# Gradient clipping by norm on one core: loads of all 128 partitions in row blocks of four, finer tail loads, one reduction matmul, fewer stores

## The chip, the cores and the metric

The kernel runs on one core of a Trainium2 chip. The metric is the device time of one execution in microseconds (us), lower is better. The fast runs of one kernel are spread over 0.05 to 0.75 us; times are given as medians with the range. The profile is one execution with the hardware profiler; its span is 1.8 us shorter than the time of the same run. On one core the granted TensorE clock was 1.00, so it plays no part.

## The reference

```python
def setup_inputs():
    batch, dim = 512, 4096
    return {"grad": np.random.randn(batch, dim).astype(np.float32) * 10, "max_norm": 1.0}

def reference(grad, max_norm):
    norm = np.sqrt(np.sum(grad ** 2))
    scale = min(1.0, max_norm / (norm + 1e-8))
    return (grad * scale).astype(np.float32)
```

8.39 MB come in from the HBM (the memory beside the core), are held in the SBUF (the memory in the core, here as tiles of 128 partitions), and 8.39 MB go out. The copying is done by the DMA engines, 16 by the page; a load or a store is issued on a queue, here that of SyncE (SP) or of ScalarE (ACT). No output can be scaled before the last input has been squared and summed, so there are three stages in a row: load, reduction, store.

## The kernel before

Block `t` of 128 rows goes to the 128 partitions, so a partition holds four rows of 16 KB. The first block is loaded in two pieces, by partitions: 16 and 112. ScalarE squares 9/16 of the columns of each piece (the first block as one piece), VectorE the rest; each writes a partial sum per partition into `acc`. The partial sums are summed per partition and a matmul with a matrix of ones adds over the partitions; the last 256 columns are squared by VectorE alone and added by a second matmul.

```python
    gt = g.rearrange("(t p) d -> t p d", p=P)
    ot = o.rearrange("(t p) d -> t p d", p=P)
    big = sb.tile([P, T, ncols], fp32)
    in_chunks = [
        (0, 0, ncols, 0, 16),          # block, columns, partitions
        (0, 0, ncols, 16, P),
        (1, 0, ncols, 0, P),
        (2, 0, ncols, 0, P),
        (t_last, 0, 2304, 0, P),
        (t_last, 2304, mid, 0, P),     # mid = 3840
        (t_last, mid, ncols, 0, P),
    ]
    for t, c0, c1, r0, r1 in in_chunks:
        nc.sync.dma_start(out=big[r0:r1, t, c0:c1], in_=gt[t][r0:r1, c0:c1])
    # ... ScalarE and VectorE square the pieces, partial sums into acc ...
    nc.vector.tensor_scalar(out=dumm[:, 0:ai], in0=acc[:, 0:ai], ..., accum_out=rowsum)
    nc.tensor.matmul(out=psum_tot, lhsT=ones, rhs=rowsum, start=True, stop=False)
    # ... VectorE squares the last 256 columns into acc[:, ai] ...
    nc.tensor.matmul(out=psum_tot, lhsT=ones, rhs=acc[:, ai : ai + 1], start=False, stop=True)
    nc.scalar.activation(out=qv, in_=psum_tot, func=ACT.Sqrt, scale=1.0 / (mn * mn))
    nc.vector.tensor_scalar(out=rq, in0=qv, scalar1=1.0, scalar2=None, op0=OP.max)
    nc.vector.reciprocal(out=s, in_=rq)
    # ... ten pieces: VectorE ("D") or ScalarE ("A") multiplies by s,
    #     and the SP or the ACT queue stores the piece ...
```

## Time and profile before

| | before |
|---|---|
| time | 53.87 us (4 runs, 53.60 to 54.04) |
| span of the profile | 52.0 us |
| VectorE, ScalarE busy | 26%, 37% |
| input packets on the DMA engines | 1.80 to 25.84 us |
| first scaling starts | 29.17 us |
| output packets | 30.42 to 50.78 us |

The packet times are read from the DMA packets in the trace, with the first input packet put at 1.80 us here and in every later table; on the clock of the timeline they are 0.02 us earlier in this kernel. The rest is from the page and the timeline. No engine is busy half of the time: the kernel is bound by its two DMA stages and by the serial reduction between them.

The first view is the page's part 2 of the kernel before: the span in 40 slices of 1.3 us, the busy tenths of the 16 DMA engines and the GB/s that they moved. The bytes of a packet are counted in the slice in which it starts, so single slices swing about the true rate.

```profile
DMA  0997798989999999999500069999999999999980
GB/s 0 202 202 202 202 365 239 290 327 416 453 453 428 416 416 390 411 413 425 200 0 0 0 217 406 447 428 388 405 421 411 460 422 428 403 403 409 453 346 0
```

The pair has to be read together. The engines count as busy from the second slice on, but in slices 2 to 5 they move 202 GB/s and only from about the tenth on over 410. A busy DMA engine is not always one that moves data at full rate: a packet of 16,384 bytes took 0.61 to 0.65 us later on, and 0.73 to 2.14 us in the slow stretch.

The second view is the chain of work that ended last, by engine (page, part 4). SPq, ACTq and DVEq are the instruction queues of SyncE, ScalarE and VectorE, PE is the matmul engine, and "issue" is time in which nothing was waited for that the profile shows.

```profile
DMA 44%; ACT 14%; issue 5%; SPq 4%; DVE 3%; PE 2%; ACTq 1%; DVEq 0%
...
```

The third view is the DMA list of the kernel before: the input loads, their KB, and the microseconds from issue to landing. The last load (128 KB, issued at 3.5 us) lands 22.8 us later, at 26.32.

```profile
big<-in_grad_dram SPq DMA_DIRECT2D x2, 2048.0 KB, 17.0
...
big<-in_grad_dram SPq DMA_DIRECT2D x1, 1792.0 KB, 10.5
...
big<-in_grad_dram SPq DMA_DIRECT2D x1, 128.0 KB, 22.8
```

The fourth is the timeline around the end of the input: start, duration, engine, line, operation, operands, and in brackets the idle time before it with what ended it.

```profile
11.75 2.12 ACT L83 ACTIVATE sq_a<-big 128x2304 f32<-128x2304 f32 x1 [9.53 <-DMA big<-in_grad_dram]
...
26.18 0.86 DVE L89 CUSTOM_DVE_ANT_0 sq_v<-big 128x672 f32<-128x672 f32 x1 [0.81 <-DMA big<-in_grad_dram]
26.96 0.42 DVE L113 CUSTOM_DVE_ANT_0 sq_v<-big 128x256 f32<-128x256 f32 x1
27.30 0.16 DVE L101 TENSOR_SCALAR_CACHE_REDUCE dumm<-acc 128x10 f32<-128x10 f32 x1
...
27.52 0.59 PE L110 MATMUL psum_tot<-rowsum,ones 128*128 128x1 f32 x2 [27.52 <-DVE dumm L101]
27.98 0.57 PE L123 MATMUL psum_tot<-acc,ones 128*128 128x1 f32 x2
28.58 0.17 ACT L127 ACTIVATE qv<-psum_tot 128x1 f32<-128x1 f32 x1 [1.50 <-PE psum_tot L123]
...
29.17 2.83 ACT L153 ACTIVATE big<-big,s 128x512 f32<-128x512 f32 x2 [0.42 <-DVE s L129]
```

The first square starts only at 11.75 us. At the end VectorE squares 672 and then 256 columns, sums (L101), and two matmul pairs follow each other. Note that the sum over the partial sums runs after the square of the last piece, although the program has them the other way round: the scheduler changed the order, and so the split into two matmuls hides less than was meant (0.22 us, by an experiment below).

### The profile page before, as it was taken

Reading aid. Unit: us, or ns where it says so; the run is one execution under the profiler, and the core shown is the slowest. Engines: PE = TensorE matmul, PEld = TensorE weight load, DVE = VectorE, ACT = ScalarE, POOL = GpSimd, SP = SyncE. Lnnn points to the kernel's source line nnn. Section 1 sums busy time; section 2 is a strip of 40 time slices with the busy share of each in tenths; the row PEclk is TensorE's granted clock in tenths of the full one; section 3 lists DMA queues with packets and bytes.
Section 4 is the critical chain, followed back from the end, with each engine's and each line's share of the span. In section 5 each row is a group of like instructions: output and inputs, shape, how many; then the busy total and the mean of one; then the engine's idle time right before and its main releaser. Section 6 shows DMA issues by size and latency. Waiting matters only on the chain.

```text
span 52.0 us, 127 instructions
## 1 busy us (share of the span) xinstructions
PE 1.0 (2%) x4; PEld 0.9 (2%) x4; DVE 13.7 (26%) x22; ACT 19.4 (37%) x18; POOL 0.2 (0%) x4
## 2 busy tenths in 40 slices
PE   0000000000000000000007000000000000000000
PEld 0000000000000000000007000000000000000000
DVE  1000000009602930495581899900000000000000
ACT  4600000009702940595670696999770000000000
POOL 1000000000000000000000000000000000000000
DMA  0997798989999999999500069999999999999980
GB/s 0 202 202 202 202 365 239 290 327 416 453 453 428 416 416 390 411 413 425 200 0 0 0 217 406 447 428 388 405 421 411 460 422 428 403 403 409 453 346 0
DMA packets 2320, 16.78 MB, mean 322 GB/s; under 512 B 272, under 2 KB 528, under 8 KB 912
## 3 DMA queue, kind: packets, MB, share of 16 engines
q1 hardware_dynamic: 1600, 12.19, 63.5%
q10 hardware_dynamic: 720, 4.59, 21.4%
HBM read 8.39 MB, written 8.39 MB: 322 GB/s over the span
## 4 chain that ended last, share of the span: by engine, by line
DMA 44%; ACT 14%; issue 5%; SPq 4%; DVE 3%; PE 2%; ACTq 1%; DVEq 0%
DMA big<-in_grad_dram 44%; ACT big L153 13%; SPq L75 4%; DVE sq_v L89 2%; ACTq L159 1%; PE psum_tot L110 1%; PE psum_tot L123 1%; ACT qv L127 0%; DVE s L129 0%; DVE rq L128 0%; DVE dumm L101 0%; DVE acc L113 0%; DVE sq_v L113 0%; DVEq L89 0%; DVE acc L89 0%
## 5 line engine op out<-in xcount | busy, mean ns | idle before, releaser
L83 ACT ACTIVATE sq_a<-big 128x2304 f32<-128x2304 f32 (+2 forms) x5 | 8.6, 1716 | 15.8 <-DMA big<-in_grad_dram 15.8
L89 DVE CUSTOM_DVE_ANT_0 sq_v<-big 128x1792 f32<-128x1792 f32 (+2 forms) x5 | 8.1, 1628 | 17.9 <-DMA big<-in_grad_dram 17.9
L153 ACT ACTIVATE big<-big,s 128x2048 f32<-128x2048 f32 (+2 forms) x5 | 8.7, 1783 | 1.3 <-ACT big L153 0.8
L161 DVE TENSOR_SCALAR big<-big,s 128x2048 f32<-128x2048 f32 (+2 forms) x5 | 4.6, 990 | 0.0
L77 ACT ACT_TABLE_LOAD x1 | 1.3, 1283 | 0.7 <-PEq L185 0.7
L110 PE MATMUL psum_tot<-rowsum,ones 128*128 128x1 f32 x2 | 0.6, 363 | 27.5 <-DVE dumm L101 27.5
L110 PEld LDWEIGHTS psum_tot<-rowsum,ones 128*128 128x128 f32 x2 | 0.5, 313 | 27.5 <-DVE dumm L101 27.5
L83 ACT ACTIVATION_READ_ACCUMULATOR sq_a<-big 128x1 f32 x5 | 0.9, 187 | 0.0
L127 ACT ACTIVATE qv<-psum_tot 128x1 f32<-128x1 f32 x1 | 0.2, 171 | 1.5 <-PE psum_tot L123 1.5
L123 PE MATMUL psum_tot<-acc,ones 128*128 128x1 f32 x2 | 0.6, 352 | 0.0
L123 PEld LDWEIGHTS psum_tot<-acc,ones 128*128 128x128 f32 x2 | 0.6, 336 | 0.0
L128 DVE TENSOR_SCALAR rq<-qv 128x1 f32<-128x1 f32 x1 | 0.2, 155 | 1.3 <-ACT qv L127 1.3
L113 DVE CUSTOM_DVE_ANT_0 sq_v<-big 128x256 f32<-128x256 f32 x1 | 0.4, 420 | 0.0
L89 DVE DVE_READ_ACCUMULATOR2_ANT acc<- 128x1 f32 x5 | 0.4, 82 | 0.0
L72 DVE MEMSET ones<- 128x128 f32 x1 | 0.2, 165 | 0.8 <-PEq L185 0.8
L77 ACT ACTIVATE junk<-ones 1x1 f32<-1x1 f32 x1 | 0.2, 203 | 0.0
L129 DVE RECIPROCAL s<-rq 128x1 f32<-128x1 f32 x1 | 0.2, 163 | 0.0
L101 DVE TENSOR_SCALAR_CACHE_REDUCE dumm<-acc 128x10 f32<-128x10 f32 x1 | 0.2, 158 | 0.0
L185 POOL MEMSET const-bfloat16-1.0<- 128x1 bf16 x1 | 0.1, 102 | 0.0
L185 POOL MEMSET const-uint8-127<- 128x1 uint8 x1 | 0.1, 102 | 0.0
L185 POOL MEMSET const-float32-0.0<- 128x1 f32 x1 | 0.1, 100 | 0.2 <-issue 0.2
L185 POOL MEMSET const-float32-1.0<- 128x1 f32 x1 | 0.1, 99 | 0.0
(2 smaller groups left out, 0.2 us busy)
## 6 DMA issues: line engine op xcount, KB each, us to landing
big<-in_grad_dram SPq DMA_DIRECT2D x2, 2048.0 KB, 17.0
out_dram<-big SPq DMA_DIRECT2D x3, 1024.0 KB, 9.7
out_dram<-big ACTq DMA_DIRECT2D x3, 1024.0 KB, 12.3
big<-in_grad_dram SPq DMA_DIRECT2D x1, 1792.0 KB, 10.5
big<-in_grad_dram SPq DMA_DIRECT2D x1, 1152.0 KB, 21.6
out_dram<-big ACTq DMA_DIRECT2D x1, 1152.0 KB, 8.2
big<-in_grad_dram SPq DMA_DIRECT2D x1, 768.0 KB, 23.0
out_dram<-big SPq DMA_DIRECT2D x1, 512.0 KB, 3.1
```

The source lines that it names most:

```text
L72: nc.vector.memset(ones, 1.0)
L75: nc.sync.dma_start(out=big[r0:r1, t, c0:c1], in_=gt[t][r0:r1, c0:c1])
L77: nc.scalar.activation(out=junk, in_=ones[0:1, 0:1], func=ACT.Sqrt)
L83: nc.scalar.activation(out=sq_a[:, c0:m], in_=big[:, t, c0:m], func=ACT.Square, accum_out=acc[:, ai : ai + 1],)
L89: nc.vector.tensor_tensor_reduce(out=sq_v[:, m:c1], in0=big[:, t, m:c1], in1=big[:, t, m:c1], scale=1.0, scalar=0.0, op0=OP.mult, op1=OP.a ...
L110: nc.tensor.matmul(out=psum_tot, lhsT=ones, rhs=rowsum, start=True, stop=False)
L113: nc.vector.tensor_tensor_reduce(out=sq_v[:, c0:c1], in0=big[:, t, c0:c1], in1=big[:, t, c0:c1], scale=1.0, scalar=0.0, op0=OP.mult, op1=O ...
L123: nc.tensor.matmul(out=psum_tot, lhsT=ones, rhs=acc[:, ai : ai + 1], start=False, stop=True)
L153: nc.scalar.activation(out=big[:, t, c0:c1], in_=big[:, t, c0:c1], func=ACT.Copy, scale=s,)
L159: nc.scalar.dma_start(out=ot[t][:, c0:c1], in_=big[:, t, c0:c1])
L161: nc.vector.tensor_scalar(out=big[:, t, c0:c1], in0=big[:, t, c0:c1], scalar1=s, scalar2=None, op0=OP.mult,)
L185: nc = _bacc.Bacc("TRN2", target_bir_lowering=False, num_devices=1)
```

## The change

It gives each partition four consecutive rows, one run of 64 KB in the HBM; cuts the columns of this run into eight loads, all over 128 partitions; makes the last ones narrower (448 and 192 columns instead of 1,536 and 256) with an own split between the engines; sums once and uses one matmul; and stores seven pieces instead of ten. The intent is to load the first block as fast as the later ones (over 410 GB/s) and to shorten what follows the last landing. The whole diff also adds a memset, moves a first square root ahead of the loads and has a branch that is never taken. The core of the diff, cut at "..." and with two lines in words:

```diff
-    gt = g.rearrange("(t p) d -> t p d", p=P)
-    ot = o.rearrange("(t p) d -> t p d", p=P)
+    gb = g.rearrange("(p k) d -> p (k d)", p=P)
+    ob = o.rearrange("(p k) d -> p (k d)", p=P)
...
-    in_chunks = [
-        (0, 0, ncols, 0, 16),
-        (0, 0, ncols, 16, P),
-        (1, 0, ncols, 0, P),
-        (2, 0, ncols, 0, P),
-        (t_last, 0, 2304, 0, P),
-        (t_last, 2304, mid, 0, P),
-        (t_last, mid, ncols, 0, P),
-    ]
+    in_chunks_plan = [            # columns, and how many of them ScalarE squares
+        (0, 4608, 2560),
+        (4608, 8704, 2304),
+        (8704, 12288, 2048),
+        (12288, 13568, 704),
+        (13568, 14848, 640),
+        (14848, 15744, 320),
+        (15744, 16192, 128),
+        (16192, W, 0),
+    ]
...
-    nc.tensor.matmul(out=psum_tot, lhsT=ones, rhs=rowsum, start=True, stop=False)
-    ... square of the last 256 columns ...
-    nc.tensor.matmul(
-        out=psum_tot, lhsT=ones, rhs=acc[:, ai : ai + 1], start=False, stop=True
-    )
+    nc.tensor.matmul(out=psum_tot, lhsT=ones, rhs=rowsum, start=True, stop=True)
...
-    out_chunks: ten pieces of 256 to 2304 columns
+    out_chunks: list[tuple[int, int, str]] = [
+        (0, 256, "D"), (256, 1088, "D"), (1088, 2368, "A"), (2368, 4416, "D"),
+        (4416, 7552, "A"), (7552, 11648, "D"), (11648, W, "A"),
+    ]
```

## The prediction

> What bounds it now. The transfers, in two phases with a serial reduction between them. The chain of waits gives 44% to the input DMA. In the timeline and the DMA packets: the first input packet starts at 1.80 us, the last ends at 25.84, it has landed at about 26.34; the first scaling starts at 29.17; the first output packet starts at 30.42, the last ends at 50.78; the span ends at 52.03 (measured time 1.84 more). VectorE (26%) and ScalarE (37%) wait.
>
> Input, 24.0 us. The page's slices show 202 GB/s in slices 2 to 5 and 239 to 327 up to about 11 us, then 416 to 453, though the DMA engines count as busy throughout. By packets: those of 16,384 bytes take 0.8 to 2.1 us before 11 us and 0.61 to 0.62 after. The slow stretch is the first block, loaded as 16 and 112 partitions. [...] I take this to be the cause; the trace agrees in that both partial-partition DMAs are slow and every full one runs at 420 to 430 GB/s.
>
> The change removes these two: all eight loads cover 128 partitions. Packet time read from the trace is about 8 ns + bytes x 0.037 ns (1,024 bytes 46 ns, 16,384 bytes 615). Eight rounds of 18,432, 16,384, 14,336, 5,120, 5,120, 3,584, 1,792 and 768 bytes make 19.9 us (estimate). Input lands at about 22.4 instead of 26.34: 3.9 us saved, all on the chain.
>
> Reduction, 2.83 us from landing to scaling. The last load falls from 256 to 192 columns, the one before from 1,536 to 448. VectorE's 672-column square (0.86 us), which was still running when the last data landed, becomes 320 columns (about 0.48). One matmul pair instead of two saves about 0.45 us, since the second ended 0.44 us after the first. Square, sum, matmul, square root, maximum and reciprocal: about 2.0 us after landing. 0.8 us saved; scaling starts at 24.4.
>
> Output, 20.35 us of packets. Still 8.39 MB and all 128 partitions, already near 420 GB/s. Seven DMAs instead of ten, larger packets: eight rounds of 1,024, 3,328, 5,120, 8,192, 12,544, 16,384 and 18,944 bytes are 19.9 us against 20.1 by the same formula: 0.25 us saved, with about 0.1 us lost where the second store waits for an 832-column scaling. Engines scale faster than the DMA drains, so the larger pieces cost nothing. The extra memset, the reordered square root and the unused split branch cost nothing on the chain.
>
> The row pitch becomes 64 KB per partition. [...] I take it as free.
>
> Sum: span 52.0 - 3.9 - 0.8 - 0.15 = 47.15; time 49.0 us, range 48.2 to 50.4. Faster 0.94, same 0.03, slower 0.03.
>
> Right if: slices reach 410 to 450 GB/s from about 2 us on; large packets take 27 bytes/ns from the first; first square starts near 8 us instead of 11.7; input lands at 22 to 22.8; landing to scaling about 2.0 us; output packets last 20 us without a gap; the span is near 47.
>
> Wrong if: the slow start is a cold start of the HBM side [...], so that the first 18 KB packets stay over 0.8 us (up to 4 us of gain lost); the 64 KB pitch slows reads or writes; rows over 16 KB are cut into less efficient pieces; the first stores leave the DMA idle; or scheduling moves a late square behind another wait.

## The result, and the profile after

| | before | after |
|---|---|---|
| time | 53.94 us (16 runs, 53.60 to 54.35) | 49.96 us (11 runs, 49.88 to 50.38) |
| span of the profile | 52.0 | 48.3 |
| input packets | 1.80 to 25.84 | 1.80 to 22.86 |
| last input landed | 26.32 | 23.25 |
| first scaling starts | 29.17 | 25.54 |
| output packets | 30.42 to 50.78 (20.35) | 26.83 to 47.11 (20.28) |

The ratio is 0.927 (95% interval 0.9245 to 0.9301). A ratio is the mean time of one kernel's fast runs over that of the other's in the same rounds, so it is not quite the ratio of the medians in the table. Executions over 1.5% slower than the fastest of the same kernel are left out of the means. The time of 49.96 us lies in the range that was predicted (48.2 to 50.4), about 1 us above the predicted 49.0.

The same views of the kernel after. Page, part 2 (slices of 1.2 us):

```profile
DMA  0969899999999989995000799999999999997950
GB/s 0 229 260 458 351 443 417 434 434 434 409 416 475 428 338 428 417 396 183 0 0 0 255 410 441 407 432 477 383 383 463 477 383 428 502 424 330 502 251 0
```

From the fourth slice to the eighth the rate is 420 GB/s on average (458, 351, 443, 417, 434); before got there at the tenth. Slices 2 and 3, at 229 and 260, are still slow. Page, part 4:

```profile
DMA 40%; ACT 18%; SPq 5%; DVE 4%; issue 1%; PE 1%; ACTq 1%; DVEq 0%
...
```

The DMA list: the last load (96 KB, issued at 4.15 us) lands 19.1 us after its issue, at 23.25.

```profile
big<-in_grad_dram SPq DMA_DIRECT2D x1, 2304.0 KB, 8.2
...
big<-in_grad_dram SPq DMA_DIRECT2D x1, 96.0 KB, 19.1
```

The timeline:

```profile
9.00 2.34 ACT L80 ACTIVATE sq_a<-big 128x2560 f32<-128x2560 f32 x1 [6.77 <-DMA big<-in_grad_dram]
...
22.50 0.76 DVE L90 CUSTOM_DVE_ANT_0 sq_v<-big 128x576 f32<-128x576 f32 x1 [0.35 <-DMA big<-in_grad_dram]
...
23.19 0.49 DVE L90 CUSTOM_DVE_ANT_0 sq_v<-big 128x320 f32<-128x320 f32 x1
...
23.60 0.35 DVE L90 CUSTOM_DVE_ANT_0 sq_v<-big 128x192 f32<-128x192 f32 x1
...
24.10 0.17 DVE L103 TENSOR_SCALAR_CACHE_REDUCE dumm<-acc 128x15 f32<-128x15 f32 x1
...
24.33 0.58 PE L112 MATMUL psum_tot<-rowsum,ones 128*128 128x1 f32 x2 [24.33 <-DVE dumm L103]
24.95 0.17 ACT L114 ACTIVATE qv<-psum_tot 128x1 f32<-128x1 f32 x1 [1.52 <-PE psum_tot L112]
...
25.54 4.37 DVE L142 TENSOR_SCALAR big<-big,s 128x256 f32<-128x256 f32 x4
```

VectorE has no idle time before the squares of 320 and 192 columns (no bracket): it was still at 576 and 320 when their data came. The reduction, from the last landing to the first scaling, takes 25.54 - 23.25 = 2.29 us instead of 29.17 - 26.32 = 2.85.

So of the 3.63 us by which scaling starts earlier, 3.07 come from the input and 0.56 from the reduction; the output adds almost nothing.

### The profile page after: what moved, and what is told of

Read it like the earlier page. It is cut to its first block, busy times and chain, and to the rows that moved or that the text cites. A ratio compares the mean times of both kernels' runs of the same rounds, so it can differ in the third digit from the quotient of the medians.

```text
span 48.3 us, 117 instructions
## 1 busy us (share of the span) xinstructions
PE 0.6 (1%) x2; PEld 0.5 (1%) x2; DVE 14.2 (29%) x26; ACT 19.2 (40%) x20; POOL 0.2 (0%) x4
## 3 DMA queue, kind: packets, MB, share of 16 engines
HBM read 8.39 MB, written 8.39 MB: 347 GB/s over the span
## 4 chain that ended last, share of the span: by engine, by line
DMA 40%; ACT 18%; SPq 5%; DVE 4%; issue 1%; PE 1%; ACTq 1%; DVEq 0%
DMA big<-in_grad_dram 40%; ACT big L134 17%; SPq L73 5%; DVE sq_v L90 3%; PE psum_tot L112 1%; ACTq L140 1%; DVE dumm L103 0%; ACT qv L114 0%; DVE s L116 0%; DVE rq L115 0%; DVE acc L90 0%; DVEq L103 0%; ACTq L134 0%
## 5 line engine op out<-in xcount | busy, mean ns | idle before, releaser
L80 ACT ACTIVATE sq_a<-big 128x2560 f32<-128x2560 f32 (+6 forms) x7 | 8.7, 1238 | 12.0 <-DMA big<-in_grad_dram 12.0
L90 DVE CUSTOM_DVE_ANT_0 sq_v<-big 128x576 f32<-128x576 f32 (+6 forms) x8 | 9.0, 1158 | 13.9 <-DMA big<-in_grad_dram 13.9
L134 ACT ACTIVATE big<-big,s 128x1280 f32<-128x1280 f32 (+2 forms) x3 | 8.4, 2834 | 0.9 <-DVE s L116 0.5
L142 DVE TENSOR_SCALAR big<-big,s 128x256 f32<-128x256 f32 (+3 forms) x4 | 4.4, 1156 | 0.0
```

Of the source, the lines that this page charges most:

```text
L80: nc.scalar.activation(out=sq_a[:, oa : oa + wa], in_=big[:, c0 : c0 + wa], func=ACT.Square, accum_out=acc[:, ai : ai + 1],)
L90: nc.vector.tensor_tensor_reduce(out=sq_v[:, ov : ov + wd], in0=big[:, c0 + wa : c1], in1=big[:, c0 + wa : c1], scale=1.0, scalar=0.0, op0 ...
L134: nc.scalar.activation(out=big[:, c0:c1], in_=big[:, c0:c1], func=ACT.Copy, scale=s[:],)
L142: nc.vector.tensor_scalar(out=big[:, c0:c1], in0=big[:, c0:c1], scalar1=s[:], scalar2=None, op0=OP.mult,)
```

## The experiments

Runs of eleven kernels were made (ten variants and the kernel after again), each with the kernel before on the same chip. All gave correct results. The theory (P): a load of part of the partitions is slow, and this alone made the start of before slow. The rivals: the first 2 MB are slow whatever their shape (S), or the new row order and the longer rows bring the gain (L).

The rates in this table were worked out from the DMA packets in the traces (bytes spread evenly over the duration of each packet): GB/s in each microsecond from 2 to 14 us, with the first packet put at 1.80 us in each kernel. On the timeline's clock the first packet came at 1.71 to 1.78 us, but at 2.05 and 2.08 in the two kernels that load the first block as halves, whose rows are thus moved by 0.25 and 0.28.

```
                    2-3  3-4  4-5  5-6  6-7  7-8  8-9 9-10  -11  -12  -13  -14
before              202  163  167  271  288  307  291  277  284  383  428  429
rows only           199  169  195  278  316  299  279  275  288  385  428  429
merged              185  266  414  432  432  430  431  432  432  431  429  432
split in 2nd block  179  277  418  430  432  376  149  122  140  192  267  278
64 + 64             273  223  206  206  212  222  210  205  206  227  338  429
even + odd          218  370  412  424  432  429  431  432  432  432  430  431
after               218  351  408  408  433  432  430  432  431  432  431  430
after, 16 + 112     158  166  157  210  272  286  293  281  270  261  300  417
after, two loads    236  365  421  429  433  431  432  435  433  435  433  435
after, small first  124  280  404  391  421  432  429  432  432  432  432  429
```

### One part of the change alone: the first block in one load

```diff
-        (0, 0, ncols, 0, 16),
-        (0, 0, ncols, 16, P),
+        (0, 0, ncols, 0, P),
```

> The kernel before, with its first block loaded by one 128-partition DMA instead of 16 + 112 partitions; nothing else. Theory P ([...] this is the slow start of before): block 0 lands near 8.0 us instead of 11.7, less a start-up loss of about 0.8 us that the kernel after also showed; time 50.8 us (50.4 to 51.3). Rival S (start-up: the first 2 MB of any kernel is slow whatever its shape): 53.9. Rival L (layout: the new row order and the longer rows bring the gain): 53.9.

Measured: 50.53 us against 54.08 of before in the same rounds, ratio 0.935 (0.930 to 0.939). The first square starts at 8.37 us instead of 11.75. Page, part 2, of this kernel:

```profile
GB/s 0 202 202 417 430 430 430 430 430 430 430 430 430 444 375 416 416 403 139 0 0 0 234 412 430 430 425 395 457 403 403 410 410 430 430 430 430 417 336 0
```

This lies in theory P's range. One part of the change brings 3.5 of the 4 us. S fails, and L is not needed. The first two microseconds remain slow (185 and 266 GB/s).

### Another part alone: the row order

```diff
-    gt = g.rearrange("(t p) d -> t p d", p=P)
-    ot = o.rearrange("(t p) d -> t p d", p=P)
+    gt = g.rearrange("(p t) d -> t p d", p=P)
+    ot = o.rearrange("(p t) d -> t p d", p=P)
```

> The kernel before with only the row order of the change (partition p gets rows 4p to 4p+3, so the pitch between partitions is 64 KB in the HBM); the 16 + 112 split stays, all sizes stay. Theory P: 53.9 us (53.5 to 54.3), block 0 still lands near 11.7. Rival S: 53.9. Rival L: near 51.

Measured: 54.18 us against 54.08, ratio 1.002 (0.996 to 1.008); the first square starts at 11.77 us. L falls: a pitch of 64 KB between partitions instead of 16 KB neither helps nor harms, for the loads and the stores of this kernel together.

### The split moved to the second block

```diff
-        (0, 0, ncols, 0, 16),
-        (0, 0, ncols, 16, P),
-        (1, 0, ncols, 0, P),
+        (0, 0, ncols, 0, P),
+        (1, 0, ncols, 0, 16),
+        (1, 0, ncols, 16, P),
```

> The kernel before with block 0 whole and block 1 loaded as 16 + 112 partitions. Theory P: block 0 lands near 8.0; the 16 KB packets of block 1 take over 0.75 us and it needs about 3 us more than blocks 2 and 3's pace of 4.9; time 53.5 us (52.8 to 54.2). Rival S: block 0 lands near 11.7 as in before, block 1 takes 4.9; 53.9. If the split costs only while the DMA starts up, both blocks are fast: 50.8.

Measured: two runs, 55.2 and 55.79 us, ratio 1.026 (1.017 to 1.035); two runs and the profile were slow (56.2 and 56.3). The profile is used only for where the slow packets lie.

```profile
GB/s 0 193 277 446 421 385 84 157 193 289 241 265 265 349 421 446 355 434 397 419 129 0 0 0 331 440 385 438 392 440 434 415 403 446 403 434 434 385 385 0
```

The slow stretch moved with the split, to the 7th to 14th slice. So it is not the start. The size was missed: the fast runs lie about 5 us above the merged version (55.5 - 50.5), not 3. In the profile the first block too was late, its square starting at 10.19 us instead of 8.37. Why it was late was not shown.

### The block in halves: 64 + 64, and every second partition

The split of the first block into equal halves asks whether the uneven numbers of rows (16 and 112: 1 and 7 for each of 16 engines, if they are spread evenly, which no trace here shows) are at fault.

```diff
-        (0, 0, ncols, 0, 16),
-        (0, 0, ncols, 16, P),
+        (0, 0, ncols, 0, 64),
+        (0, 0, ncols, 64, P),
```

> The kernel before with block 0 loaded as 64 + 64 partitions. Theory P [...] both halves move at about 215 GB/s; block 0 lands near 11.7 to 12.5 us; time 54.3 us (53.5 to 55.3). Rival U (it is the uneven or small number of rows, 1 and 7 per engine, that hurts): [...] block 0 lands near 8.0, time 50.8.

Measured: 55.05 us, ratio 1.018 (1.013 to 1.022), which is slower than before although the two loads are even (0.27 of the 0.97 us between them are a first packet that came later, 2.05 against 1.78 us). Page, part 2:

```profile
GB/s 0 197 209 209 197 283 233 209 221 233 504 455 393 393 393 455 412 408 422 386 81 0 0 79 394 412 424 408 416 418 442 436 406 399 449 430 393 436 350 0
```

Both halves move at 205 to 223 GB/s by the table (3 to 10 us), about half of the 430 of a whole load; the median packet of the block took 1.27 us instead of 0.61, and the first square starts at 13.07 us. So uneven numbers of rows are not needed for a slow load; whether they add something is not shown.

The next run asks whether every load of 64 partitions is this slow; it loads the even partitions and then the odd ones:

```diff
+    for r in (0, 1):
+        nc.sync.dma_start(out=big[r:P:2, 0, :], in_=gt[0][r:P:2, :])
     # the loop over in_chunks follows, without the two pieces of block 0
```

> The kernel before with block 0 loaded as the 64 even and then the 64 odd partitions. [...] as fast as one whole load, 50.6 us. [...] about 206 GB/s for this block as with 64 + 64, time 54 to 55.5 us.

Measured: 51.05 us, ratio 0.943 (0.940 to 0.947). Page, part 2:

```profile
GB/s 0 160 266 386 426 426 426 426 426 439 426 439 426 420 386 314 392 419 211 0 0 0 198 411 456 413 382 443 438 394 406 419 419 413 426 426 426 426 319 0
```

The block moves at 424 to 432 GB/s from 5 us on; the two loads landed one after the other, at 6.18 and 8.63 us. Two loads of 64 partitions each run at full rate (424 to 432 GB/s) or at half (205 to 223), by which partitions they are, so the number of loads and their size are ruled out as the cause. Why the two pairs differ was not shown. One rival is not tested by itself here: the halves also read other rows of the HBM, 1 MB in one piece against every second row. Against it speak the rows-only run and the split put back (below): with the rows 64 KB apart a load of 16 and 112 partitions is as slow as before (54.18 against 54.08 us, and 54.30 against 54.11). Of the two outcomes in the expectation, the second, about 206 GB/s and 54 to 55.5 us, missed. (The time is 0.5 us above the merged version: the first packet came at 2.08 instead of 1.74 us, and the slices show a dip to 314 later, which was not pursued.)

What stays open too is the load of 112 partitions: it moved at 271 to 307 GB/s in before (5 to 11 us), between the half and the full rate of the loads of 64, and no run here shows why.

### The split put back into the kernel after

```diff
     for c0, c1, _ in in_chunks:
-        nc.sync.dma_start(out=big[:, c0:c1], in_=gb[:, c0:c1])
+        for r0, r1 in [(0, 16), (16, P)] if c0 == 0 else [(0, P)]:
+            nc.sync.dma_start(out=big[r0:r1, c0:c1], in_=gb[r0:r1, c0:c1])
```

> The kernel after with its first load (now 4,608 columns) cut into 16 + 112 partitions again; all else as after. Theory P: the loss that the kernel before had over its merged version (3.5 us for 4,096 columns) comes back, about in proportion to the bytes: 53.7 us (53.0 to 54.5). If the new row order, the longer rows or the new sizes had removed the slow start by themselves: 50 us.

Measured: 54.30 us, ratio to before 1.003 (0.999 to 1.008). With this single part undone, nothing is left of the gain. The loss of 4.3 us (against the 49.96 us of the kernel after, from another call) is above the central 3.7, but the time is in the range; that a first load an eighth larger loses that much more is plausible and was not tested by itself.

### The slow start that remains: is it the queueing of later loads?

In the kernel after the first 16 packets of 18,432 bytes took 0.86 to 1.66 us instead of 0.686. Over the 16 engines, packets above this median in the first load add up to 0.76 us for each engine. The SP queue is still issuing loads at that time, until 4.6 us, so the kernel after was given only two loads.

```diff
-    for c0, c1, _ in in_chunks:
+    for c0, c1 in [(0, 4608), (4608, W)]:
         nc.sync.dma_start(out=big[:, c0:c1], in_=gb[:, c0:c1])
```

> The kernel after with two loads (columns 0 to 4607 and all the rest) instead of eight, to look at the start-up alone; it will be slower in all, about 55 us, since the squares of the rest come late. Theory C (cold start: the first reads are slow whatever is queued behind them): the rate in the microseconds 2 to 3 and 3 to 4 stays near 200 and 350 GB/s. Rival Q (queueing the later six loads, which lasts until 4.6 us, takes rate from the first): queueing ends at 1.6 us, so the rate is over 400 GB/s from 2.5 us on.

Measured, one look: 55.32 us. The rates are 236 and 365 GB/s in the microseconds 2 to 3 and 3 to 4, as after has with 218 and 351, although issuing ended at 1.6 us; the same excess is 0.58 us for each engine, where three more profiles with the first load of after (after again and the even tail twice) have 0.61 to 0.69. That agrees with theory C; issuing later loads costs little or none of it. The slow start is called a cold start below, but whether the reads or the writes are slow was not separated. All whole first loads show it, with the old row order and the new one (merged: 185 and 266); over those of 4,096 or more columns the excess is 0.6 to 0.9 us for each engine. The output stage of after showed none: its first 16 packets (1,024 bytes) took 0.046 to 0.047 us, with a median of 0.047 for all 128 of that size; but these are small.

### A small first load to take the cold start

The base is the kernel with the even tail, below.

```diff
-    for c0, c1, _ in in_chunks:
+    for c0, c1, _ in [(0, 64, 0), (64, 4608, 0)] + in_chunks[1:]:
         nc.sync.dma_start(out=big[:, c0:c1], in_=gb[:, c0:c1])
```

> The kernel with the evenly shared tail, its first load cut into a 64-column and a 4,544-column load, both of all 128 partitions. If the slow start is a delay of each engine's first access, whatever its size, the small load takes it while the second is still being queued: the first block lands up to 0.4 us earlier, 49.3 us. If instead the reads are slow until some 2 us after the first of them, or for the first 0.6 MB: no gain, or up to 0.2 us of loss for one more issue: 49.7 to 49.85.

Measured: 50.14 us (49.97 to 50.20) against 49.73 (49.62 to 49.92) for its base: 0.4 us lost, twice the most that was expected, about one issue time of the SP queue (0.44 us). The large packets started at 2.28 instead of 1.80 us (124 and 280 GB/s in the table), and were as slow as before: the first 16 took 0.76 to 1.63 us, an excess of 0.75 us for each engine. So the small load does not use up the slow start; it comes with the large transfer (the packets of 256 bytes before it took 0.015 to 0.018 us, all alike). What is cold was not found.

### One sum and one matmul alone

```diff
-    # sum of acc[:, 0:ai], matmul (start), square of the last 256 columns, matmul (stop)
+    # square of the last 256 columns, sum of acc[:, 0 : ai + 1]
+    nc.tensor.matmul(out=psum_tot, lhsT=ones, rhs=rowsum, start=True, stop=True)
```

> The kernel before with one sum over all eleven partial sums and one matmul, as the change has it; nothing else. As the prediction had it (the second matmul is 0.44 us on the chain, its removal costs nothing): 0.45 us less than before, 53.45. Rival W (the sum over the partial sums, which did not need the last square before, now waits for its accumulator to be written, about 0.2 us in the trace of the kernel after): 0.2 to 0.25 us less, 53.7.

Measured: 53.77 us against 53.83, ratio 0.9975 (0.992 to 1.003): a gain too small to be told from none by the times. In the profile the scaling starts 28.90 - 26.90 = 2.00 us after the start of the last square, in before's 29.17 - 26.96 = 2.21 us after it. The timeline:

```profile
26.90 0.42 DVE L102 CUSTOM_DVE_ANT_0 sq_v<-big 128x256 f32<-128x256 f32 x1
...
27.46 0.16 DVE L112 TENSOR_SCALAR_CACHE_REDUCE dumm<-acc 128x11 f32<-128x11 f32 x1
...
27.69 0.59 PE L121 MATMUL psum_tot<-rowsum,ones 128*128 128x1 f32 x2 [27.69 <-DVE dumm L112]
```

The sum starts 27.46 - 26.90 = 0.56 us after the start of the last square, where before had it at 27.30 - 26.96 = 0.34, while the square was ending: now it needs the accumulator of that square. The matmul pair that went was worth 0.44 us (its end at 28.55 after the first pair's at 28.11), and 0.22 us came back as this wait. The trace agrees with rival W; the times are compatible with it and decide nothing.

### The tail shared more evenly

```diff
-        (14848, 15744, 320),
-        (15744, 16192, 128),
+        (14848, 15744, 448),
+        (15744, 16192, 288),
```

> The kernel after with the squares of its two loads before the last shared more evenly (ScalarE takes 448 of 896 and 288 of 448 columns instead of 320 and 128). Theory V (VectorE's queue of three squares, 576, 320 and 192 columns, still runs when the last data has landed and sets the start of the sum): scaling starts about 0.2 us earlier after the last landing, time 0.2 us less than the kernel after (49.75). Rival (the last landing alone sets it, the queue is hidden): no change.

Its partner was the kernel after again:

> The kernel after, unchanged, so that the variants of it in the same call have a partner: 49.9 to 50.1 us.

Measured: 49.65 us (49.59 to 49.83), ratio to before 0.921 (0.917 to 0.925); the kernel after 49.97 (49.87 to 50.09), ratio 0.927. No run of one lies among those of the other; the difference of the medians is 0.32 us. Once more:

> The kernel with the evenly shared tail, unchanged, as the partner of the small-first-load variant in this call: 49.65 us (49.5 to 49.8).

It gave 49.73 us (49.62 to 49.92), ratio 0.919 (0.916 to 0.922). The timeline of the even tail:

```profile
22.44 0.62 DVE L90 CUSTOM_DVE_ANT_0 sq_v<-big 128x448 f32<-128x448 f32 x1 [0.34 <-DMA big<-in_grad_dram]
...
23.00 0.32 DVE L90 CUSTOM_DVE_ANT_0 sq_v<-big 128x160 f32<-128x160 f32 x1
...
23.24 0.35 DVE L90 CUSTOM_DVE_ANT_0 sq_v<-big 128x192 f32<-128x192 f32 x1
...
25.18 2.11 DVE L142 TENSOR_SCALAR big<-big,s 128x256 f32<-128x256 f32 x3
```

The three squares are 448, 160 and 192 columns wide, the last starts at 23.24, and scaling starts at 25.18; in the kernel after, the last starts at 23.51 and scaling at 25.45:

```profile
22.41 0.76 DVE L90 CUSTOM_DVE_ANT_0 sq_v<-big 128x576 f32<-128x576 f32 x1 [0.33 <-DMA big<-in_grad_dram]
...
23.51 0.35 DVE L90 CUSTOM_DVE_ANT_0 sq_v<-big 128x192 f32<-128x192 f32 x1
...
25.45 2.11 DVE L142 TENSOR_SCALAR big<-big,s 128x256 f32<-128x256 f32 x3
```

From the first of these squares to the start of the last it is 0.80 us here and 23.51 - 22.41 = 1.10 us there. Theory V holds: about 0.3 us was VectorE's queue. This version beats both kernels, by 0.3 us over after.

## Why the prediction was right, and where its sum was off

The direction, the cause and the range held: loading the first block in parts of the partitions was what cost. Why it cost was not shown, neither for the loads of 64 partitions nor for the 112. The sum was short by about 1 us.

1. "The slow stretch is the first block, loaded as 16 and 112 partitions". Right: merging it brings 3.5 us by itself, the split moved to the second block moves the slow stretch, the split put back undoes the gain, and halves run at half rate (205 to 223 GB/s) or at full (424 to 432), by which partitions they are. That the split is the cause is measured; the mechanism behind it is not.
2. "Eight rounds ... make 19.9 us", so that the input lands at 22.4. This term was mis-sized: the packets lasted from 1.80 to 22.86, 21.1 us, and the last landed at 23.25; the first square started at 9.00, not near 8. The sum put the settled packet time on every packet from the first. The first load's packets were slow by 0.76 us for each engine, a cold start. In before it lay inside the slow stretch, so that it could not be told from the rest. The other part is that a sum of packet times leaves out the time in which an engine has no packet: summed over the 16 engines the packets took 20.58 us for each, 0.48 less than they lasted (in before 23.66, 0.38 less). The prediction named the cold start as what would make it wrong; it was real, but 0.8 us and not the "up to 4 us" that it allowed for.
3. "About 2.0 us after landing". Measured 2.29. Two terms were too small: VectorE was still at the squares of 576 and 320 columns when the last data came (the even tail takes 0.3 us out), and "one matmul pair instead of two saves about 0.45 us" left out that the sum now waits for the last accumulator (0.21 us were left of it in the trace of that part alone). The two come to more than the 0.29 that was missed, so something else in the estimate was too large; it was not taken apart.
4. Output: "about 0.25 us saved, with about 0.1 us lost". The packets took 20.28 instead of 20.35 us. Right within 0.1 us: it moved 412 GB/s before and 414 after (8.39 MB over these times). "Engines scale faster than the DMA drains" holds here: in after ScalarE scales 128x4736 (2.42 MB) in 4.24 us, 571 GB/s.
5. The 64 KB row pitch "I take as free". Right: alone it gives a ratio of 1.002.
6. The sum: scaling was predicted at 24.4 and started at 25.54, of which 0.85 us are point 2 (landing at 23.25 instead of 22.4) and 0.29 point 3. The output stage after it was right, so the span came out at 48.3 instead of 47.15, and the time at 49.96 instead of 49.0.

## What to carry to other kernels

Cut loads along the columns and let every DMA cover all 128 partitions; a small piece of the partitions "to get started" can take much of the rate of a whole block (here 163 to 307 GB/s for its two pieces, where the later blocks had about 430; one load instead made 50.53 us of 54.08), while the DMA engines still count as busy, so read busy share and GB/s together (here 202 GB/s at a busy share of seven to nine tenths). When a sum of settled packet times is laid over the first microseconds of a kernel, add a measured start-up (here 0.6 to 0.9 us for each engine) and the time without packets (0.4 to 0.5). Where the last data decides, look at which engine still has a queue at that moment, and check in the timeline that the scheduler kept the order in which the code was written.
